# Low parts of the channel-stage weights: a negated copy by ScalarE and an adding DMA from GpSimd

## The chip, the core and the metric

The kernel runs on one core of one Trainium2 chip. TensorE multiplies matrices, VectorE (DVE) and ScalarE (ACT) do element-wise work, GpSimd (POOL) does element-wise work and can issue DMAs, SyncE (SP) issues DMAs. The metric is the device time of one execution in microseconds. A time is given as the median of several runs.

## What is computed

One layer of a decoder for 1024 prompt tokens and 8 x 4 sample tokens, 1056 in all, with 1024 features: a mixing stage (attention and pooling), a channel stage (a gated feed-forward layer with 2816 hidden features) and a last projection with a gate. The change touches the channel stage and the last projection. Cut to what matters:

```python
f = _rms(x, n_ffn_pre)
f = (jax.nn.silu(f @ w_gate) * (f @ w_up)) @ w_down
x = x + _rms(f, n_ffn_post)
x = x + jax.nn.sigmoid(x @ w_ple_gate) * (p @ w_ple)
```

All inputs and outputs are float32.

## The kernel before, in words

**Split operands.** TensorE multiplies in float32r, a rounded form of float32. To keep float32 accuracy, each operand is split in a high part (the value rounded to float32r) and a low part (the value minus its high part). A product takes three matmuls (`gemm`): high weight by high data, high weight by low data, low weight by high data, in this order for every block of 128 rows. The low weight, `wl`, is thus first read by the third matmul of its product. `split` (L163) makes the two parts: ScalarE copies the high part (L164), VectorE subtracts it from the source (L165).

**Groups.** The 1056 tokens are cut in three groups of 352 columns, 0, 1 and 2. A product of 1024 rows takes 24 matmuls of 128x352, one of 512 rows takes 12.

**Weights.** Weights are listed in `plan`, each a tile of 128 partitions x 1024 values, 512 KB. `w_load` has SyncE load one into a raw tile `wr`, of which there are three (`W_RAW`). `w_split` loads it, takes two `wp` tiles called `wh` and `wl`, and splits it. There are eight `wp` tiles (2 x `W_PAIRS`), so four pairs; a tile is written again only when TensorE has used what it held.

**Items.** From the channel stage on, weights are handed out by `ITEMS` and `need`. `need(k)` prepares all items up to `k + LOOK` (`LOOK` is 4) and loads the next two raw. An item is either "direct", one weight split as it is, or "sums": four GpSimd instructions (`w_sums`, L980) form sums of the quarters of a gate and an up weight in place, in their raw tiles, and two splits turn the results into tiles `sh` and `sl`, which also come from the `wp` tiles. With the sums, groups 0 and 1 share products and need fewer matmuls. The items hold 113 direct weights: 64 loads of `w_gu` (gate and up), 32 of `w_dn` (down), 14 of `w_pg` and 3 of `w_ple` (last projection). The 22 sums make 44 `sh`/`sl` pairs.

**Order of the work.** The hidden features are cut in 11 slabs of two chunks; a chunk is called a channel below. `WALK` goes over slabs 0 to 4 for group 2 alone, then slabs 5 to 10 for all three groups, then slabs 0 to 4 again for groups 0 and 1; the weights of slabs 0 to 4 are loaded and split twice. Meanwhile `ffn_steps` prepares groups 0 and 1 in the first part. `gate_up` does one channel; `down` multiplies a slab by its two down weights and adds the result into `o` (L1075, L1077). At the end `ple_out` does the last projection. From the attention's end on, TensorE's instructions stand in an order fixed by the program (`keep_in_program_order`); the other engines' orders follow from a scheduler. Each engine takes its queue in order, and an instruction that waits holds all behind it. In the channel stage GpSimd's queue has only the sums, and SyncE's has all weight loads.

`weights`, which serves the mixing stage, also calls `w_split`; its weights keep VectorE's subtraction in both kernels.

Of the kernel before, what the change touches and what calls it, by code (L numbers as in the profile page):

```python
# [12 lines left out]
AF = mybir.ActivationFunctionType  # L13
ALU = mybir.AluOpType
# [47 lines left out]
def trunk_kernel(  # L62
# [32 lines left out]
    te, ve, se, ge = nc.tensor, nc.vector, nc.scalar, nc.gpsimd  # L95
# [58 lines left out]
    plan = []  # L154
# [3 lines left out]
    def fix(ins):  # L158

        if fixed[0]:  # L160
            tc.keep_in_program_order(ins)

    def split(hi, lo, src):  # L163
        fix(se.copy(hi, src))  # L164
        fix(ve.tensor_tensor(lo, src, hi.bitcast(F32), op=ALU.subtract))  # L165

    raws, pairs = {}, {}

    def w_load(j):
        if j >= len(plan) or j in raws:  # L170
            return
        src, shape = plan[j]
        t = wpool.tile(shape, F32, tag="wr", bufs=W_RAW, name=nm("wr"))
        nc.sync.dma_start(t, src)
        raws[j] = t

    def w_tile(shape, s):
        return wpool.tile(shape, F32R, tag="wp", bufs=2 * W_PAIRS, name=nm(s))

    def w_split(j):  # L180
        if j >= len(plan) or j in pairs:
            return
        w_load(j)
        shape = plan[j][1]
        hi, lo = w_tile(shape, "wh"), w_tile(shape, "wl")
        split(hi, lo, raws[j])
        pairs[j] = (hi, lo)

    def weights(j, ahead=W_PAIRS - 1):
        for i in range(j, j + ahead + 1):  # L190
            w_split(i)
            w_load(i + 1)
        return pairs[j]
# [22 lines left out]
    def item(kind, *js):  # L216
        ITEMS.append((kind, js))
        return len(ITEMS) - 1
# [5 lines left out]
    for s, gs in WALK:  # L224
        pairs_of = []
        for i in range(SLAB):
# [9 lines left out]
            js = item("sums", jg, ju) if 0 in gs else None  # L236
# [25 lines left out]
    def need(k, ahead=LOOK):  # L262

        for i in range(len(made), min(k + ahead + 1, len(ITEMS))):
            kind, js = ITEMS[i]
            if kind == "direct":
                w_split(js[0])
                made[i] = pairs[js[0]]
            else:
                made[i] = w_sums(*(raws[ITEMS[j][1][0]] for j in js))  # L270
            for kind, js in ITEMS[i + 1 : i + 3]:
                if kind == "direct":
                    w_load(js[0])
        return made[k]
# [679 lines left out]
    for m in range(4, KC):  # L954
        out_proj(m, 1)
        need(0, m - 4)
        turn(24)
# [12 lines left out]
    def w_sums(a1, a2):  # L970


        a11, a12, a21, a22 = a1[:, 0:4, :], a1[:, 4:8, :], a2[:, 0:4, :], a2[:, 4:8, :]
        for out, a, b, op in (
            (a22, a21, a22, ALU.add),
            (a21, a11, a21, ALU.subtract),
            (a11, a22, a11, ALU.subtract),
            (a12, a12, a11, ALU.subtract),
        ):
            ge.tensor_tensor(out, a, b, op=op)  # L980
        two = []
        for src in (a1, a2):
            hl = w_tile([P, KC, P], "sh"), w_tile([P, KC, P], "sl")
            split(*hl, src)
            two.append(hl)
        (s24, s31) = two
        return {"S2": quarter(s24, 0), "S4": quarter(s24, 1), "S3": quarter(s31, 0), "S1": quarter(s31, 1)}
# [8 lines left out]
    def gate_up(items, slot, gs, pending):  # L996
# [16 lines left out]
        def add(out, a, ps):  # L1013
            ve.tensor_tensor(out, a, ps, op=ALU.add)  # L1014

        wg = need(ig)
        if 0 in gs:
            p1 = tmp(n, "p1")
# [8 lines left out]
        if pending and 0 in gs:  # L1027
            pending()
        wu = need(iu)
        if 2 in gs:  # L1030
            ve.tensor_tensor(sl, sl, direct(wu), op=ALU.mult)
# [234 lines left out]
```

## Time and profile before

| What | Value |
|---|---|
| Median of three runs | 1124.63 us (1122.67 to 1124.66) |
| Profiled execution, its own time | 1121.84 us |
| Its span, first to last instruction | 1120.1 us |
| TensorE busy | 1108.9 us |
| VectorE busy | 748.4 us |
| ScalarE busy | 440.7 us |
| GpSimd busy | 179.5 us |
| Read from device memory | 88.30 MB |

Engine times are taken from one profiled execution. In the page and the views, a row of a group gives line, engine, operation, output and input tiles with the buffer numbers left out, shape, count, and after the bar the busy time in us, the mean of one in ns, and the engine's idle time before them with what ended it. "PE b L126 <- DVE o L1107: 1.2, 1, 1.2" reads: TensorE, writing b at line 126, waited for VectorE's o of line 1107; us in total, times, longest. A row of the windows gives the window, its length, the busy time and count of each engine in it, the granted TensorE clock, the mean busy share of the 16 DMA engines, and GB/s. A row of the timeline gives start and length in us, engine, line and operation, and in brackets the idle time before it. A row of DMA issues gives out and in, the queue, the count, the KB of one, and the median us from issue to landing; the DMA queue's row gives packets, MB, and the time of its packets as a share of 16 engines' span. A source row gives shortest, median and longest in ns, and the first and last start in us.

### The profile page before, as it was taken

The page shows a single profiled execution, that of the slowest core. Times are in us where ns is not written, and L with a number is a line of the kernel's source. Part 1 is how long each engine was busy: PE and PEld are TensorE (multiplying, and loading weights), DVE is VectorE, ACT ScalarE, POOL GpSimd, SP SyncE. Part 2 cuts the span into 40 slices and gives each one's busy share as a digit, 9 for nine tenths or more (in the row PEclk, how much of TensorE's full clock was granted, in tenths as well). Part 3 has the DMA queues.
Part 4 walks back from the last instruction along what each step waited for, and adds up shares of the span by engine and source line. Part 5 has one row for each costly group of instructions (what it writes and reads, how often), then busy time and mean ns, then how long its engine had stood idle before and what let it go on. Part 6 is the DMA issues. An engine that isn't in the chain of part 4 may idle for free.

```text
span 1120.1 us, 17702 instructions
## 1 busy us (share of the span) xinstructions
PE 1108.9 (99%) x7171; PEld 1090.8 (97%) x7171; DVE 748.4 (67%) x1244; ACT 440.7 (39%) x782; POOL 179.5 (16%) x152
## 2 busy tenths in 40 slices
PE   8999999999999999999999999999999999999998
PEld 8999988899999999999999999999999999999998
DVE  6667468985879955355554555557887877789532
ACT  8323276664646524331321314124424334366220
POOL 0045132200000041011111101111132123100000
PEclk9999999999999999999999999999999999999999
DMA  8121311272543312111110212112212222246211
GB/s 288 57 70 43 119 41 38 83 265 71 206 159 132 114 38 76 39 61 54 38 57 20 75 38 76 39 39 93 104 57 77 74 76 79 96 161 215 91 58 39
DMA packets 35265, 99.54 MB, mean 89 GB/s; under 512 B 4180, under 2 KB 14708, under 8 KB 35184
## 3 DMA queue, kind: packets, MB, share of 16 engines
q1 hardware_dynamic: 33856, 96.65, 25.6%
q10 hardware_dynamic: 1328, 1.77, 0.5%
q8 instruction: 56, 0.92, 0.4%
q14 instruction: 25, 0.20, 0.1%
HBM read 88.30 MB, written 10.11 MB: 88 GB/s over the span
## 4 chain that ended last, share of the span: by engine, by line
PE 88%; DVE 6%; ACT 3%; DMA 1%; issue 1%; POOL 0%; SPq 0%; DVEq 0%; ACTq 0%; POOLq 0%
PE b L126 88%; ACT a L634 1%; DVE wl L165 1%; DMA xr<-in_x_dram 1%; DVE mx L626 1%; DVE a L671 1%; ACT wh L164 1%; POOL wr L980 0%; DVE h L366 0%; PE b L120 0%; DMA c<-in_gains_dram 0%; DVE o L1107 0%; DVE x L1111 0%; DVE a L734 0%; DVE p L1014 0%
## 5 line engine op out<-in xcount | busy, mean ns | idle before, releaser
L126 PE MATMUL b<-fh,wh 128*128 128x352 f32 x808 | 260.7, 323 | 0.0
L126 PE MATMUL b<-fh,wl 128*128 128x352 f32 x808 | 259.3, 321 | 0.0
L126 PE MATMUL b<-fl,wh 128*128 128x352 f32 x808 | 259.0, 321 | 0.0
L126 PE MATMUL b<-hid,wh 128*128 128x352 f32 x1056 | 252.5, 322 | 1.7 <-DVE o L1107 1.2
L164 ACT CAST wh<-wr 128x1024 fp32r<-128x1024 f32 (+1 forms) x139 | 142.9, 1030 | 249.6 <-PE b L126 206.6
L165 DVE TENSOR_TENSOR wl<-wr,wh 128x1024 fp32r<-128x1024 f32 (+1 forms) x139 | 171.7, 1238 | 63.8 <-ACT wh L164 63.6
L126 PEld LDWEIGHTS b<-hid,wh 128*128 128x128 f32 x1056 | 182.3, 188 | 2.5 <-issue 1.5
L126 PE MATMUL b<-hid,wl 128*128 128x352 f32 x528 | 169.0, 320 | 0.0
L980 POOL TENSOR_TENSOR wr<-wr 128x512 f32<-128x512 f32 x44 | 63.4, 1441 | 622.3 <-DVE wl L165 451.8
L126 PEld LDWEIGHTS b<-fl,wh 128*128 128x128 f32 x808 | 151.8, 188 | 0.0
L126 PEld LDWEIGHTS b<-fh,wl 128*128 128x128 f32 x808 | 151.8, 188 | 0.0
L126 PEld LDWEIGHTS b<-fh,wh 128*128 128x128 f32 x808 | 151.6, 188 | 0.0
L1077 DVE TENSOR_TENSOR o<-o,b 128x352 f32<-128x352 f32 x240 | 114.7, 514 | 27.3 <-PE b L126 27.2
L126 PE MATMUL b<-fh,sh 128*128 128x352 f32 x352 | 113.6, 323 | 0.0
L126 PE MATMUL b<-fl,sh 128*128 128x352 f32 x352 | 112.8, 320 | 0.0
L126 PE MATMUL b<-fh,sl 128*128 128x352 f32 x352 | 112.7, 320 | 0.0
L126 PE MATMUL b<-h,wh 128*128 128x352 f32 x480 | 106.1, 327 | 1.3 <-ACT h L364 0.9
L165 DVE TENSOR_TENSOR sl<-wr,sh 128x1024 fp32r<-128x1024 f32 x44 | 53.7, 1222 | 75.5 <-ACT sh L164 75.5
L126 PEld LDWEIGHTS b<-hid,wl 128*128 128x128 f32 x528 | 99.0, 187 | 0.0
L164 ACT CAST sh<-wr 128x1024 fp32r<-128x1024 f32 x44 | 45.7, 1047 | 130.9 <-POOL wr L980 91.3
L126 PEld LDWEIGHTS b<-h,wh 128*128 128x128 f32 x480 | 82.6, 190 | 2.6 <-DVE h L366 1.3
L126 PE MATMUL b<-h,wl 128*128 128x352 f32 x240 | 66.3, 325 | 0.0
(150 smaller groups left out, 1593.3 us busy)
## 6 DMA issues: line engine op xcount, KB each, us to landing
wr<-in_w_gu_dram SPq DMA_DIRECT2D x64, 512.0 KB, 3.3
wr<-in_w_dn_dram SPq DMA_DIRECT2D x32, 512.0 KB, 3.5
wr<-in_w_pg_dram SPq DMA_DIRECT2D x14, 512.0 KB, 3.7
x<-in_x_dram SPq DMA_DIRECT2D x6, 704.0 KB, 7.7
x1d<-x SPq DMA_DIRECT2D x6, 704.0 KB, 3.5
x<-x1d SPq DMA_DIRECT2D x6, 704.0 KB, 6.2
out_y_dram<-yo SPq DMA_DIRECT2D x24, 176.0 KB, 1.8
wr<-in_w_out_b_dram SPq DMA_DIRECT2D x8, 512.0 KB, 3.3
```

The lines of the kernel that those rows point to most:

```text
L126: ins = te.matmul(*args, **kw)
L164: fix(se.copy(hi, src))
L165: fix(ve.tensor_tensor(lo, src, hi.bitcast(F32), op=ALU.subtract))
L626: ve.tensor_reduce(mx, t, axis=AX.X, op=ALU.max)
L634: se.activation(t[:, c, :], t[:, c, :], AF.Exp, bias=nmx[:, c : c + 1], scale=scale, accum_out=sm[:, c : c + 1])
L671: ve.copy_predicated(tk, m4(0).bitcast(mybir.dt.int32), v4(cur[kv]))
L980: ge.tensor_tensor(out, a, b, op=op)
L1077: ve.tensor_tensor(o, o, v, op=ALU.add)
```

## The change

`w_split` gets a second way, used by every direct item of `need`, 113 weights: ScalarE copies the high part, then writes the negated raw weight, rounded, into the low tile; then a DMA issued by GpSimd reads the weight from device memory again and adds it onto what lies in the low tile. The rounded negated weight is the negated high part, so the sum is the low part. VectorE's subtraction is gone for these weights. The sums (`sh`, `sl`) and the mixing stage keep it. The raw load into `wr` stays, and TensorE's instructions and their order are the same. In GpSimd's queue the 113 DMA issues stand among the sums: the issue of a channel's up weight comes ahead of that channel's four sums.

```diff
--- before.py
+++ after.py
@@ -177,13 +177,19 @@
     def w_tile(shape, s):
         return wpool.tile(shape, F32R, tag="wp", bufs=2 * W_PAIRS, name=nm(s))
 
-    def w_split(j):
+    def w_split(j, by_dma=False):
         if j >= len(plan) or j in pairs:
             return
         w_load(j)
         shape = plan[j][1]
         hi, lo = w_tile(shape, "wh"), w_tile(shape, "wl")
-        split(hi, lo, raws[j])
+        if by_dma:
+
+            se.copy(hi, raws[j])
+            se.activation(lo, raws[j], AF.Copy, scale=-1.0)
+            ge.dma_start(lo, plan[j][0], accum_op=ALU.add)
+        else:
+            split(hi, lo, raws[j])
         pairs[j] = (hi, lo)
 
     def weights(j, ahead=W_PAIRS - 1):
@@ -264,7 +270,7 @@
         for i in range(len(made), min(k + ahead + 1, len(ITEMS))):
             kind, js = ITEMS[i]
             if kind == "direct":
-                w_split(js[0])
+                w_split(js[0], True)
                 made[i] = pairs[js[0]]
             else:
                 made[i] = w_sums(*(raws[ITEMS[j][1][0]] for j in js))
```

## The prediction

> **What bounds the kernel now.** I read the page first: busy times, then the chain that ended last.
>
> ```profile
> span 1120.1 us, 17702 instructions
> PE 1108.9 (99%) x7171; PEld 1090.8 (97%) x7171; DVE 748.4 (67%) x1244; ACT 440.7 (39%) x782; POOL 179.5 (16%) x152
> PE 88%; DVE 6%; ACT 3%; DMA 1%; issue 1%; POOL 0%; SPq 0%; DVEq 0%; ACTq 0%; POOLq 0%
> q1 hardware_dynamic: 33856, 96.65, 25.6%
> ```
>
> TensorE is busy in all but 11.2 us and holds 88% of the chain. The change adds and removes no matmul and leaves their order alone, so it can win only waits of TensorE, and it loses when a low part arrives after TensorE wants it. Next come the windows, cut where the walk over the slabs changes: from 264 slabs of group 2 alone ("first part"), from 403 all three groups, from 760 groups 0 and 1 ("third part"), from 1003 the last projection.
>
> ```profile
> core 0: us, PE busy (x) PEld busy (x) DVE busy (x) ACT busy (x) POOL busy (x), PEclk, DMA share, GB/s
> 264.00:403.00 139.00, 139.00 (x890) 138.88 (x889) 117.19 (x158) 75.50 (x96) 8.44 (x4) 1.00 0.41 137
> 403.00:760.00 357.00, 357.00 (x2249) 357.00 (x2248) 191.41 (x316) 99.28 (x152) 58.53 (x44) 1.00 0.15 50
> 760.00:1003.00 243.00, 241.19 (x1520) 240.17 (x1518) 193.98 (x315) 96.79 (x139) 55.57 (x40) 1.00 0.27 88
> 1003.00:1120.00 117.00, 112.19 (x702) 111.65 (x702) 63.99 (x99) 34.95 (x51) 0.00 (x0) 0.99 0.31 110
> PE b L126 <- DVE o L1107: 1.2, 1, 1.2
> PE b L126 <- DVE hid L165: 0.5, 1, 0.5
> PE b L126 <- DVE dg L310: 0.4, 1, 0.4
> ```
>
> The last three rows are all of TensorE's waits from 264 on: 2.1 us, each ended by VectorE, and the granted clock is 0.99 to 1.00. So **the most that a freed VectorE can give is 2.1 us**, 0.19% of the time, even if every one of these waits goes.
>
> **What is removed.** The 113 subtractions of direct weights leave VectorE:
>
> ```profile
> L165 DVE TENSOR_TENSOR wl<-wr,wh 128x1024 fp32r<-128x1024 f32 x113 | 137.6, 1220 | 48.8 <-ACT wh L164 48.6
> L164 ACT CAST wh<-wr 128x1024 fp32r<-128x1024 f32 x113 | 118.5, 1049 | 214.3 <-PE b L126 177.5 <-issue 31.7 <-DMA wr<-in_w_pg_dram 2.7
> ```
>
> VectorE loses 137.6 us that lay under TensorE. I put the gain at 0; its bounds are 0 and 2.1 us.
>
> **What is added on ScalarE.** 113 more passes over 128x1024. The nearest row is the high-part copy above, 1.05 us (a multiplying pass and a copy are alike at 1408 columns: 1377 and 1371 ns):
>
> ```profile
> L893 ACT ACTIVATE y<-x 128x1408 f32<-128x1408 f32 x4 | 5.5, 1377 | 0.7 <-DVE x L892 0.7
> L164 ACT CAST fh<-y 128x1408 fp32r<-128x1408 f32 x9 | 12.3, 1371 | 2.6 <-DVE y L939 1.8 <-DVE y L903 0.8
> ```
>
> That is 118.5 us, at most 32 x 1.05 = 34 us on 75.5 of 139 in the first part, where 32 of the weights are split. ScalarE has the room. What is queued behind a negated copy (a SiLU, a copy out of PSUM) is 1.05 us later; the eight banks in rotation take that up, since each is filled by 12 or 24 matmuls of 139.00/890 = 0.156 us (1.9 or 3.7 us). Cost 0; without that cover, up to 1 us a channel.
>
> **What is added on the DMA engines.** Each weight is now read twice: the plain load into wr stays, and the adding transfer reads the same 512 KB again. From the first fence, 25.6% of 1120.1 us moved 96.65 MB, 2.97 us per MB, so a plain 512 KB (0.524 MB) fills all 16 engines for 1.56 us. No adding transfer is in the trace. Its lower bound is 1.56 us, as a load. It must also read what lies in wl, and then write: if none of these three passes overlaps, 3 x 1.56 = 4.7 us. I take two, 3.1 us: a plain load reads and writes within its 1.56, so only the second read is extra. In the first part the engines were busy 0.41 x 139 = 57 us. With 32 more transfers this becomes 57 + 50 = 107, 57 + 99 = 156, or 57 + 150 = 207 us of 139. At my value the engines fall 17 us behind. The cover found below (11.7 us from ScalarE's start to first use, less a need of 9.5) takes 2 to 3 of these: **14 us lost in the first part**, bounds 0 and 66. In the second (0.15) and third (0.27) parts the engines stay under full even at 4.7 us: 34 weights each, 34 x 4.7 = 160 us on 66 of 243 in the third.
>
> The Trainium skill (Collectives: The Full Stack, The bandwidth ceiling) says that an adding DMA runs at half a copy's rate because both its sources are read through one ring, 62.28 against 32.35 GB/s. By that ratio of 1.93 the transfer takes 3.0 us here and the first part loses 11 instead of 14. No run here shows it yet.
>
> **What is added in time to arrival.** The rings set the cover: four pairs of wp tiles, so a high part can start only when the pair four places back has been used. These rows are ScalarE's start on wh and TensorE's first read of the matching wl (the third matmul of its product):
>
> ```profile
> 312.91 1.06 ACT L164 CAST wh<-wr 128x1024 fp32r<-128x1024 f32 x1 [1.14 <-issue]
> 324.59 0.32 PE L126 MATMUL b<-hid,wl 128*128 128x352 f32 x1
> ...
> 606.66 1.06 ACT L164 CAST wh<-wr 128x1024 fp32r<-128x1024 f32 x1 [4.56 <-PE b L126]
> 618.34 0.32 PE L126 MATMUL b<-fh,wl 128*128 128x352 f32 x1
> ...
> 757.29 1.05 ACT L164 CAST wh<-wr 128x1024 fp32r<-128x1024 f32 x1 [4.56 <-PE b L126]
> 765.15 0.32 PE L126 MATMUL b<-hid,wl 128*128 128x352 f32 x1
> ...
> 848.14 1.05 ACT L164 CAST wh<-wr 128x1024 fp32r<-128x1024 f32 x1
> 855.07 0.32 PE L126 MATMUL b<-fh,wl 128*128 128x352 f32 x1
> ...
> 891.70 1.04 ACT L164 CAST wh<-wr 128x1024 fp32r<-128x1024 f32 x1
> 898.46 0.32 PE L126 MATMUL b<-fh,wl 128*128 128x352 f32 x1
> ...
> 932.22 1.04 ACT L164 CAST wh<-wr 128x1024 fp32r<-128x1024 f32 x1
> 940.41 0.32 PE L126 MATMUL b<-fh,wl 128*128 128x352 f32 x1
> ...
> 980.57 1.05 ACT L164 CAST wh<-wr 128x1024 fp32r<-128x1024 f32 x1
> 987.12 0.32 PE L126 MATMUL b<-hid,wl 128*128 128x352 f32 x1
> ...
> 1014.01 1.04 ACT L164 CAST wh<-wr 128x1024 fp32r<-128x1024 f32 x1
> 1020.46 0.32 PE L126 MATMUL b<-fh,wl 128*128 128x352 f32 x1
> ```
>
> The first two pairs are typical of the first and second parts, 11.7 us. The other six are the tight places: 7.9, 6.9, 6.8, 8.2, 6.5 and 6.5 us. Before, wl needed 1.05 + 1.22 us. Now it needs two passes of ScalarE, 2.1 us, and then the time from GpSimd's issue to landing. Rows near that:
>
> ```profile
> wr<-in_w_gu_dram SPq DMA_DIRECT2D x64, 512.0 KB, 3.3
> x<-in_x_dram SPq DMA_DIRECT2D x6, 704.0 KB, 7.7
> L980 POOL TENSOR_TENSOR wr<-wr 128x512 f32<-128x512 f32 x44 | 63.4, 1441 | 622.3 <-DVE wl L165 451.8 <-DMA wr<-in_w_gu_dram 168.8
> ```
>
> The load of this size lands after 3.3 us. I add 1.56 for the second read, 1.0 for GpSimd to issue (not in the trace; from below 0, from above one of its 1.44 us instructions), and 1.56 for a plain load sharing the engines: 7.4 us, close to the 7.7 of the loads that queue behind others. The need is 2.1 + 7.4 = 9.5 us. The six places are short by 1.6, 2.6, 2.7, 1.3, 3.0 and 3.0: **14 us lost at the tight places**. The low bound is 3.3 + 1.0 = 4.3, need 6.4, nothing lost. The high bound is three passes beside a load, 3.3 + 3.1 + 1.0 + 1.56 = 9.0, need 11.1: short by 3.2, 4.2, 4.3, 2.9, 4.6 and 4.6, 24 us.
>
> **What is queued behind the waiting issue.** GpSimd takes its queue in order, so its four sums of a channel (L980, now L986) stand behind the issue of that channel's up weight, which waits for the negated copy. They needed VectorE's subtraction before (1.22), ScalarE's pass now (1.05), so they start 0.2 us earlier plus the issue, 1.0: 0.8 late. The cover is in the third part:
>
> ```profile
> 970.51 1.23 DVE L165 TENSOR_TENSOR sl<-wr,sh 128x1024 fp32r<-128x1024 f32 x1 [1.84 <-ACT sh L164]
> 974.73 0.32 PE L126 MATMUL b<-fh,sl 128*128 128x352 f32 x1
> ```
>
> From 971.74 to 974.73 is 3.0 us, so it costs nothing until an issue holds GpSimd for 3.2 us. The wr tile of a down or last-projection weight comes free 0.2 us earlier; SyncE's next load gains nothing that TensorE sees.
>
> **The sum.** 14 + 14 = 28 us, all of it waits of TensorE. The profiled execution took 1121.8 us (its span and 1.7 around it) and becomes 1150. The median shown, 1124.6, is 2.8 above that execution, so I forecast 1153.
>
> **Rivals.**
> *Hidden.* An adding transfer costs little more than a load: landing 4.3 us, 1.56 us of engines. It decides below a need of 6.5, where none of the eight pairs is late and the first part's engines hold 107 of 139 us. Then only VectorE's relief is left: 1122.5 to 1124.6, faster than before if all three waits go. For it: DMA share 0.15 to 0.41, covers mostly 11.7 us. Against: something must read the old wl. The Trainium skill (DMA: Bandwidth & Descriptors, Anatomy of one DMA) fits a GpSimd-issued DMA as 2.0 us plus bytes over 436 GB/s; plain that is 3.2 (the trace has 3.3 from SyncE), with twice the bytes 4.4 and 2.4 of engine time, which would fit this case: 57 + 77 = 134 of 139.
> *Three passes.* 66 + 24 = 90 us: 1215. For it: a transfer that reads, adds and writes back may overlap nothing. Against: plain loads do overlap reading with writing.
> *GpSimd holds each issue long*, say 6 us, writing the transfer. Sums are late by 2.8 in the third part's ten channels, 28 us; landing becomes 12.4, need 14.5: in the first part 2.8 us at every fourth of 32 weights, 22 us, and at the six places 6.6, 7.6, 7.7, 6.3, 8.0 and 8.0, 44 us: 1219. For it: GpSimd is slow (1.44 us for a half-tile sum). Against: SyncE issues the like in 0.33 us.
>
> ```profile
> L174 SPq DMA_DIRECT2D wr<-in_w_gu_dram x61: 327/328/328, 267.4 to 950.8; - x61
> ```
>
> **How the numbers follow.** A difference under 0.2%, 2.2 us, can't be told from none. Chances: forecast 0.52 (own range 1128 to 1185: landing 5.5 to 8.5 us, engines 2 to 3.8 us), hidden 0.14, three passes 0.24, held issue 0.10. Hidden splits into 0.04 faster, 0.07 same and 0.03 slower; all else is slower: 0.04, 0.07, 0.89. The range runs from 1126, a need of 6.9 with the first part hidden, to 1225, just past the two slow rivals; about 0.1 lies below and 0.1 above.
>
> **What would show it.** Right: L126 waits on a DMA of wl, most between 264 and 403 with the DMA share near 1, and again near the six places; landing about 7 us; VectorE some 138 us less, ScalarE 118 us more. Wrong: no waits on wl (hidden); waits of about equal size through 403 to 760 (landing over 9.6 us); sl late with GpSimd busy before it (held issue); a longer matmul where nothing waits.

## The result, and the profile after

| | Before | After |
|---|---|---|
| Median of four runs | 1123.78 us (1122.67 to 1124.66) | 1165.43 us (1164.06 to 1175.34) |
| Ratio of times, 95% interval | | 1.039 (1.035 to 1.043) |
| Profiled execution, its own time | 1121.84 us | 1166.63 us |
| Its span | 1120.1 us | 1164.9 us |

The change made the kernel slower by 41.7 us. The forecast was 1153, within 1126 to 1225: the sign and the range held, the size was 12 us short. First the page of the kernel after, the lines that answer to those of before:

```profile
span 1164.9 us, 18006 instructions
PE 1126.2 (97%) x7171; PEld 1102.6 (95%) x7171; DVE 646.8 (56%) x1131; ACT 543.3 (47%) x895; POOL 276.4 (24%) x265
q0 software_dynamic: 16272, 59.25, 28.1%
issue 46%; PE 27%; POOL 15%; DVE 4%; DMA 4%; ACT 3%; POOLq 0%; SPq 0%; ACTq 0%; DVEq 0%
```

TensorE ran the same 7171 matmuls, but they took 17.3 us longer (1126.2 against 1108.9), and its idle time grew from 11.2 to 38.7 us. So there are two losses to look for: waits, and matmuls that were themselves slower. The queue q0 is new: 113 adding transfers, 0.281 x 1164.9 / 113 = 2.90 us of all 16 engines each. The chain of waits is of little use here: 46% of it is "issue", time for which the profile shows no reason, since it wanders into GpSimd's queue. TensorE is still busy 97% of the span, so its own waits and its windows are the views to trust.

The windows of the kernel after, cut at the same moments as before, except that the last is longer:

```profile
core 0: us, PE busy (x) PEld busy (x) DVE busy (x) ACT busy (x) POOL busy (x), PEclk, DMA share, GB/s
264.00:403.00 139.00, 131.97 (x821) 129.30 (x820) 79.16 (x121) 99.04 (x120) 26.96 (x31) 0.99 0.97 249
403.00:760.00 357.00, 357.00 (x2233) 357.00 (x2232) 170.28 (x277) 126.74 (x182) 92.55 (x81) 1.00 0.44 98
760.00:1003.00 243.00, 233.43 (x1450) 230.72 (x1449) 148.66 (x251) 115.52 (x153) 81.30 (x71) 1.00 0.60 142
1003.00:1164.00 161.00, 144.85 (x871) 142.81 (x869) 67.86 (x126) 67.84 (x95) 16.45 (x19) 0.95 0.65 165
```

In the first part the DMA share went from 0.41 to 0.97: the engines are full, and TensorE is idle for 7.0 us. In the second part TensorE is busy without a gap. In the third it misses 9.6 us, in the last window 16 (4.8 before, with the same tail behind the last matmul), and there the granted clock is 0.95. These are TensorE's longest waits, grouped by what ended them:

```profile
PE b L126 <- DMA wl<-in_w_dn_dram: 9.0, 7, 2.8
PE b L126 <- DMA wl<-in_w_pg_dram: 8.1, 2, 5.4
PE b L126 <- DMA wl<-in_w_gu_dram: 6.2, 6, 2.6
PE b L126 <- DVE dg L316: 2.8, 2, 1.8
PE b L126 <- DMA wl<-in_w_ple_dram: 2.6, 1, 2.6
```

Sixteen waits on the adding transfer, 25.9 us; before there was none on a DMA. The DMA issues of the kernel after (the last number is the median from issue to landing), with the store `x1d` as a bystander:

```profile
wr<-in_w_gu_dram SPq DMA_DIRECT2D x64, 512.0 KB, 4.9
wl<-in_w_gu_dram POOLq DMA_DIRECT2D x64, 512.0 KB, 7.0
wl<-in_w_dn_dram POOLq DMA_DIRECT2D x32, 512.0 KB, 8.7
wl<-in_w_pg_dram POOLq DMA_DIRECT2D x14, 512.0 KB, 8.2
x1d<-x SPq DMA_DIRECT2D x6, 704.0 KB, 13.6
```

An adding transfer lands after 7.0 to 8.7 us, and plain loads suffer with it: 4.9 us where the same load took 3.3. ScalarE waits 29.5 us in all for plain loads of `w_gu` and `w_dn` before its high-part copies (0.5 in the kernel before), which shortens the cover of what it then splits.

**Where the 44.8 us between the two profiled spans arise.** Both programs give TensorE the same instructions in the same order, so the n-th matmul on a split weight can be set beside the n-th of before, and the difference of their starts tells how late TensorE runs. Its growth, worked out from the timelines of both traces, with before's times as borders of the parts (980 rather than 1003, so that the tight place at 980.57 falls to the end), is:

```
growth of the lateness, us     first 264-403   second 403-760   third 760-980   end 980-1115
kernel after                       11.2             2.5             10.7            18.5
forecast                           14               0                8.2             6
```

Another 1.8 us lie before 264, where the two programs do the same work. The forecast's fourteen at tight places are 8.2 in the third part and 6.0 at the end. Three of four parts came out within 3 us; the end is 12.5 us too small, which is most of the 16.6 us by which the forecast for the profiled execution, 1150, fell short.

The forecast took all of its 28 us to be waits of TensorE. The waits on `wl` are 25.9 us, but not where they were put: 6.8 in the first part (14 forecast), 8.4 in the third (8.2) and 10.7 at the end (6). The other 19 us are losses that no term of the sum had; they are taken apart below.

### The profile page after: what moved, and what is told of

Its sections match the earlier page's. It is cut to its first block, busy times and chain, and to the rows that moved or that the text cites. A ratio compares the mean times of both kernels' runs of the same rounds, so it can differ in the third digit from the quotient of the medians.

```text
span 1164.9 us, 18006 instructions
## 1 busy us (share of the span) xinstructions
PE 1126.2 (97%) x7171; PEld 1102.6 (95%) x7171; DVE 646.8 (56%) x1131; ACT 543.3 (47%) x895; POOL 276.4 (24%) x265
## 4 chain that ended last, share of the span: by engine, by line
issue 46%; PE 27%; POOL 15%; DVE 4%; DMA 4%; ACT 3%; POOLq 0%; SPq 0%; ACTq 0%; DVEq 0%
PE b L126 27%; POOL wr L986 10%; POOL wl L190 5%; DMA wl<-in_w_pg_dram 2%; DMA wl<-in_w_dn_dram 2%; ACT a L640 1%; DMA xr<-in_x_dram 1%; DVE wl L165 1%; DVE mx L632 1%; DVE a L677 1%; DVE acc L789 0%; ACT wh L164 0%; DMA c<-in_gains_dram 0%; DVE h L372 0%; PE b L120 0%
## 5 line engine op out<-in xcount | busy, mean ns | idle before, releaser
L126 PE MATMUL b<-fh,wl 128*128 128x352 f32 x808 | 264.5, 327 | 14.4 <-DMA wl<-in_w_pg_dram 8.1
L126 PE MATMUL b<-fh,wh 128*128 128x352 f32 x808 | 263.9, 327 | 0.0
L126 PE MATMUL b<-fl,wh 128*128 128x352 f32 x808 | 262.4, 325 | 0.0
L188 ACT CAST wh<-wr 128x1024 fp32r<-128x1024 f32 x113 | 118.4, 1048 | 227.8 <-PE b L126 175.5
L126 PEld LDWEIGHTS b<-fh,wl 128*128 128x128 f32 x808 | 155.1, 192 | 17.3 <-DMA wl<-in_w_pg_dram 8.7
L190 POOL DMA_DIRECT2D wl<-in_w_gu_dram x64 | 56.0, 874 | 458.6 <-ACT wl L189 408.4
L126 PEld LDWEIGHTS b<-fl,wh 128*128 128x128 f32 x808 | 154.6, 191 | 0.0
L126 PEld LDWEIGHTS b<-fh,wh 128*128 128x128 f32 x808 | 154.3, 191 | 0.0
L189 ACT ACTIVATE wl<-wr 128x1024 fp32r<-128x1024 f32 x113 | 119.1, 1054 | 0.0
L126 PEld LDWEIGHTS b<-hid,wl 128*128 128x128 f32 x528 | 99.6, 189 | 11.8 <-DMA wl<-in_w_dn_dram 11.7
L986 POOL TENSOR_TENSOR wr<-wr 128x512 f32<-128x512 f32 x44 | 66.1, 1502 | 1.7
## 6 DMA issues: line engine op xcount, KB each, us to landing
x1d<-x SPq DMA_DIRECT2D x6, 704.0 KB, 13.6
```

Source lines behind the costliest of these rows:

```text
L126: ins = te.matmul(*args, **kw)
L188: se.copy(hi, raws[j])
L189: se.activation(lo, raws[j], AF.Copy, scale=-1.0)
L190: ge.dma_start(lo, plan[j][0], accum_op=ALU.add)
```

## The experiments

Each kernel is the changed one with the edit shown; its time is compared with before's median on the same chip, which lay between 1122.61 and 1124.82 us, and the interval of the ratio is 95%. Four restrict the adding DMA to parts of the walk; all other direct weights get VectorE's subtraction back. `PART[k]` is the number of items before entry k of `WALK`; `AHEAD` is the end of the first part and `NSLAB` that of the second.

### One part at a time

**First part alone.**

```diff
-                w_split(js[0], True)
+                w_split(js[0], i < PART[AHEAD])
```

> The adding DMA serves only the 30 direct weights of the first part of the walk (group 2 alone); all later direct weights keep VectorE's subtraction. Transfer theory (16 DMA engines full in the first part, late arrival in the third part and at the end, and the lower clock after those waits): 10 to 13 us over the kernel before, 1134 to 1137 us, DMA share above 0.9 between 264 and 403 and no wait on wl after 420. ScalarE theory (its second pass over each weight is what delays): about 30/113 of the 42 us, 11 us, but with TensorE waits ended by ScalarE and spread evenly.

Measured: 1132.29 us, 1.0076 (1.0061 to 1.0091), 8.5 us more. TensorE waits three times on `wl`, 5.5 us; in the lateness the first part grew by 9.0 and the rest by less than 0.3. The loss is real, if smaller than the 10 to 13 us that I expected (the edit reaches 28 weights, not 30), and what is lost there isn't won back later.

**Second part alone.**

```diff
-                w_split(js[0], True)
+                w_split(js[0], PART[AHEAD] <= i < PART[NSLAB])
```

> The adding DMA serves only the direct weights of the second part (all three groups). Transfer theory: no TensorE wait on wl at all, 1123 to 1127 us; the upper end if the 0.65% longer matmuls of that part in the changed kernel come from the transfers, the lower end if they came with that execution. ScalarE theory: 34/113 of 42 us, 12 us, so 1136.

Measured: 1123.6 us, 1.000 (0.999 to 1.001). The DMA issues of this kernel:

```profile
wl<-in_w_gu_dram POOLq DMA_DIRECT2D x24, 512.0 KB, 5.9
wl<-in_w_dn_dram POOLq DMA_DIRECT2D x12, 512.0 KB, 8.8
```

And its second part's window:

```profile
403.00:760.00 357.00, 357.00 (x2249) 357.00 (x2248) 173.30 (x281) 127.58 (x182) 87.02 (x76) 1.00 0.42 97
```

Thirty-six transfers, whose median landing goes up to 8.8 us, cost nothing where the cover is 11.7 us and the engines have room, and the same 2249 matmuls as before fit in the window. It also shows what a freer VectorE is worth in this part: nothing.

**Third part and end.**

```diff
-                w_split(js[0], True)
+                w_split(js[0], i >= PART[NSLAB])
```

> The adding DMA serves only the direct weights of the third part and of the last projection. Transfer theory: 26 to 32 us over the kernel before, 1150 to 1156, with single waits of 1 to 5 us on wl and lower granted clock after 1003. ScalarE theory: about 49/113 of 42 us, 18 us, 1142. If the three single-part kernels add up to 42 us, the parts do not feed each other.

Measured: 1154.12 us, 1.0273 (1.0244 to 1.0301), 30.4 us more: 20.5 us of waits on `wl`, and 17 us in which the granted clock was one half (in part of it TensorE still waited, as is shown below for the changed kernel). The three parts nearly add: 8.5 + 0 + 30.4 = 38.9 of 41.7 us.

**Third part without the end.**

```diff
-                w_split(js[0], True)
+                w_split(js[0], PART[NSLAB] <= i < PART[-1])
```

> The adding DMA serves only the third part, without the last two down weights and the last projection. If the parts do not feed each other: 10 to 12 us, 1134 to 1136, which leaves 19 of the 30 us of the third-part-and-end kernel to the end. If the end's waits come from what the third part leaves behind in the queues: more than 15 us, waits on DMAs after 980 although no weight there is added onto.

Measured: 1136.11 us, 1.0118 (1.0103 to 1.0133), 13.5 us more, just over what I expected; of it 9.1 in six waits on `wl`, of which those of 1.82 and 2.45 us were each followed by 3.4 us at half clock. After 980 nothing more is lost, so the third part alone leaves nothing behind for the end: the other 30.4 - 13.5 = 16.9 us arise at the end. A kernel that changes the end alone was not run.

### What the transfer costs

**Copy in place of add.** The low part then holds the whole weight, so the kernel computes something else; only its time counts.

```diff
-            ge.dma_start(lo, plan[j][0], accum_op=ALU.add)
+            ge.dma_start(lo, plan[j][0])
```

> The GpSimd DMA copies the weight over the low tile instead of adding onto it, so the low part holds the whole weight; path, issue and order are those of the changed kernel. If the second read of an adding transfer is the price: engines 1.5 to 1.6 us for a transfer instead of 2.9, landing 4.5 to 5.5 us instead of 7 to 9, no wait in the first part (107 of 139 us) and under 3 us in all: 1123 to 1128. If the issue from GpSimd and its fixed time are the price: landing stays over 6.5 us and 1145 or more.

Measured: 1136.67 us, 1.0109 (1.0080 to 1.0138). The adding queue's row on the page of this kernel, now a copying one, and its DMA issues:

```profile
q0 software_dynamic: 16272, 59.25, 15.8%
wl<-in_w_gu_dram POOLq DMA_DIRECT2D x64, 512.0 KB, 4.2
```

Its window of the first part:

```profile
264.00:403.00 139.00, 139.00 (x890) 138.77 (x889) 84.66 (x129) 103.68 (x127) 22.36 (x36) 1.00 0.76 260
```

And TensorE's longest wait on the copies, by group:

```profile
PE b L126 <- DMA wl<-in_w_pg_dram: 5.1, 2, 3.9
```

A copy takes 0.158 x 1133.0 / 113 = 1.58 us of the engines, a plain load's 1.56; the addition doubles it, lengthens the median landing from 4.2 to 7.0 us for `w_gu` and is worth 29.8 us (41.7 over before for the change, 11.9 for this kernel). The first part then loses nothing and the third 1.4 us. But the end still loses 11 us: there even a copy is late, though its need, 2.1 + 5.0 (the landing of a `w_pg` copy) = 7.1 us, should miss the cover of 6.5 by 0.6. The miss of the expectation lies there: the copy behind the wait of 3.9 us, issued at 1022.6, landed after 8.2 us, not 5.0.

**Add from the raw tile in SBUF** rather than from device memory.

```diff
-            ge.dma_start(lo, plan[j][0], accum_op=ALU.add)
+            ge.dma_start(lo, raws[j], accum_op=ALU.add)
```

> The adding DMA reads the raw tile on the chip instead of device memory; the raw tile then stays taken until the transfer lands. If reading device memory twice is the price: engine time and landing fall to those of a copy, 1124 to 1132. If two reads are the price wherever they come from: engine time near 2.9 us again, and with three raw tiles held some 7 us longer the plain loads come later, 1165 to 1200.

Measured: 1237.01 us, 1.0998 (1.0973 to 1.1024). The adding queue's row on its page:

```profile
q0 software_dynamic: 16272, 59.25, 26.2%
```

And TensorE's two longest groups of waits:

```profile
PE b L126 <- DMA wl<-wr: 27.1, 19, 4.7
PE b L126 <- DVE o L1083: 24.3, 11, 4.0
```

A transfer takes 0.262 x 1232.2 / 113 = 2.86 us, like the 2.90 of the add from device memory. So adding doubles the engines' time wherever its source lies. That a second read is the reason fits this, but no run separates reading from adding. The kernel is slowest of all, and slower than the 1165 to 1200 that I expected: the raw tile is now held until the transfer has landed, so SyncE's next loads wait for these transfers, 77 times and 484 us in all, and ScalarE waits 107 us for the loads.

**The traffic without the data path.** VectorE splits as before, and an adding DMA of the same size, from the finished low part to a buffer in device memory that nobody reads, runs beside it.

```diff
-            se.copy(hi, raws[j])
-            se.activation(lo, raws[j], AF.Copy, scale=-1.0)
-            ge.dma_start(lo, plan[j][0], accum_op=ALU.add)
+            split(hi, lo, raws[j])
+            spare.append(dpool.tile([P, *shape[1:]], F32, name=nm("spare")))
+            ge.dma_start(spare[-1], lo.bitcast(F32), accum_op=ALU.add)
```

> VectorE's subtraction makes the low part as before; besides, GpSimd issues an adding DMA of 512 KB for each direct weight, from the finished low part onto a buffer in device memory that nothing reads. So the engines' load is there and no product waits for it. If late arrival through the ring is what costs: nothing outside the first part, and there only what the plain loads are late by, 0 to 8 us, 1124 to 1132. If the load on the engines alone costs (the plain loads come late): 20 us or more, TensorE waiting behind ScalarE's wait on wr.

Measured: 1153.04 us, 1.0262 (1.0237 to 1.0287). ScalarE's waits on loads in this kernel:

```profile
ACT wh L164 <- DMA wr<-in_w_gu_dram: 40.6, 22, 4.3
ACT wh L164 <- DMA wr<-in_w_dn_dram: 11.5, 6, 3.2
```

No matmul waits for these transfers, and 28 us are lost all the same: the plain loads come late (before, ScalarE waited 0.5 us for loads of `w_gu` and `w_dn`, here 52.1), and once VectorE waits 2.6 us for a low slot that a transfer still reads. I had expected 0 to 8 us; the load on the engines counts for more than the forecast allowed outside the first part. It isn't the changed kernel's loss taken alone, since a low slot here is held by VectorE's pass and the transfer together.

**Half a transfer.** The DMA adds onto the first half of the low tile; VectorE subtracts in the other.

```diff
-            se.activation(lo, raws[j], AF.Copy, scale=-1.0)
-            ge.dma_start(lo, plan[j][0], accum_op=ALU.add)
+            n = shape[1] // 2
+            se.activation(lo[:, :n], raws[j][:, :n], AF.Copy, scale=-1.0)
+            ge.dma_start(lo[:, :n], plan[j][0][:, :n], accum_op=ALU.add)
+            ve.tensor_tensor(lo[:, n:], raws[j][:, n:], hi[:, n:].bitcast(F32), op=ALU.subtract)
```

> Only the first half of each low tile is made by the negated copy and the adding DMA; VectorE subtracts the second half. Transfer theory: the time follows the size of the transfer. Engines 1.4 to 1.5 us each, so the first part is not full (57 + 28 x 1.45 = 98 of 139 us) and loses nothing; landing 5.5 to 6 us, need about 7.4, so places with 6.5 to 6.9 us of cover are short by 0.5 to 0.9 and no wait is long enough to lower the clock: 1125 to 1131. If a fixed price of each issue from GpSimd or of each ScalarE pass decides, half a transfer costs nearly what a whole one does: 1145 or more.

Measured: 1145.52 us, 1.0207 (1.0187 to 1.0226). TensorE's waits:

```profile
PE b L126 <- DVE o L1085: 5.4, 3, 2.5
PE b L126 <- DMA wl<-in_w_pg_dram: 3.4, 2, 2.5
PE b L126 <- DVE hid L165: 1.7, 1, 1.7
```

The first part loses next to nothing (0.3 us), as a transfer of 1.57 us of the engines should. The rest is a miss of my theory: waits on `wl` fell to 5.3 us, but new waits on VectorE, 5.4 and 1.7 us, came in their place, and 13.7 us passed at half clock. Splitting the work over three engines brought new waits here rather than removing them.

### What ScalarE's pass costs

**The pass without the DMA.** ScalarE writes the negated copy, VectorE adds the raw weight.

```diff
-            ge.dma_start(lo, plan[j][0], accum_op=ALU.add)
+            ve.tensor_tensor(lo, raws[j], lo.bitcast(F32), op=ALU.add)
```

> ScalarE writes the negated copy as in the changed kernel, but VectorE then adds the raw weight onto it; there is no second transfer. Transfer theory: 0 to 3 us over the kernel before (need 2.1 + 1.2 us against covers of 6.5 and more), 1124 to 1127, ScalarE some 118 us busier. ScalarE theory: most of the 42 us stays, 1150 or more.

Measured: 1136.2 us, 1.0101 (1.0082 to 1.0121). The group of VectorE's additions in this kernel:

```profile
L190 DVE TENSOR_TENSOR wl<-wr,wl 128x1024 fp32r<-128x1024 f32 x113 | 138.3, 1224 | 93.7 <-ACT wl L189 93.4
```

And TensorE's waits:

```profile
PE b L126 <- DVE o L1083: 4.5, 3, 2.3
PE b L126 <- DVE hid L165: 2.8, 2, 2.6
```

The pass isn't free in general: 11.4 us, where I expected 0 to 3. But, as far as these waits show, the mechanism is one that the changed kernel doesn't have. VectorE stands 93.4 us before its additions, waiting for ScalarE's second pass (48.6 before, for the first), and holds the work for `o` and `hid` behind it. In the changed kernel VectorE has no low part to wait with, and TensorE's waits on those two together are 1.2 us.

**Negated copy and issue first.**

```diff
-            se.copy(hi, raws[j])
             se.activation(lo, raws[j], AF.Copy, scale=-1.0)
             ge.dma_start(lo, plan[j][0], accum_op=ALU.add)
+            se.copy(hi, raws[j])
```

> ScalarE writes the negated copy and GpSimd's issue follows before ScalarE copies the high part, so each adding transfer starts about 1.05 us earlier and nothing else changes. Transfer theory: each wait of the third part and the end is about 1 us shorter, the first part stays (its engines are full): 1148 to 1158. ScalarE theory: the same work on ScalarE, no gain, 1163 to 1167.

Measured: 1159.89 us, 1.0327 (1.0310 to 1.0345), 36.1 us over before where the change has 41.7, so some 5.5 us less, a little less of a gain than I expected. Waits on `wl` fell from 25.9 to 13.7 us; in their place:

```profile
PE b L126 <- DVE o L1083: 3.6, 4, 1.3
PE b L126 <- DVE hid L165: 2.3, 4, 0.6
```

So 1.05 us on the way to the landing is worth 12 us of those waits, and 5.9 us of waits on VectorE's `o` and `hid` give half of it back.

**High part by VectorE**, so that ScalarE has one pass only.

```diff
-            se.copy(hi, raws[j])
+            ve.tensor_copy(hi, raws[j])
```

> VectorE copies the high part, ScalarE only writes the negated copy, so ScalarE makes one pass for each weight as in the kernel before and the adding transfer is issued 1.05 us earlier than in the changed kernel. Transfer theory: the first part still loses 8 to 11 us, the third part and the end lose 1 us less at each of their 8 to 10 waits: 1150 to 1158. If the second pass in ScalarE's queue is the larger half of the loss: 1140 or less. If no gain over 1162: neither, and the copy on VectorE holds GpSimd up.

Measured: 1159.86 us, 1.0337 (1.0319 to 1.0354), 37.3 us over before, some 4.4 us less than the change, which the intervals don't quite tell apart; I expected more. VectorE's copy takes 0.69 us; landing stays at 7.5 to 9.1 us, and 21.8 us of waits on `wl` remain. By these two kernels ScalarE's extra pass is worth some 5 us in the changed kernel. That the adding makes most of the rest is shown by the copy in place of it, which took away 29.8. None of these kernels beats the one before; the only one that equals it uses the adding DMA in the second part alone.

## Why the forecast was right, and where it was short

**TensorE bounds, and a freed VectorE gives nothing.** Held. VectorE's busy time fell by 101.6 us and no time came back: where the DMA cost nothing, in the second part alone, the time is 1123.6.

**ScalarE's passes cost nothing.** Nearly. The row is 1054 ns x 113 = 119.1 us, as forecast (ScalarE's busy time rose by 102.6 only, since passes that follow each other overlap by 0.1 us), and no wait of the changed kernel names them. Taking a pass out of the transfer's way won 4.4 to 5.5 us, in two ways; the forecast had this pass in its need of 2.1 us.

**The engines fill in the first part.** Held. I took two reads, 3.1 us; the page shows 2.90, a copy 1.58, an add from SBUF 2.86. The share of 0.97 is the full engine that 156 us of work in 139 foretold, and 11.2 us were lost (8.5 alone) where 14 were forecast. The forecast had them all as waits; the waits are 6.8. The lateness arises in two ways: the adding transfer lands after 8.8 us in the median, and the plain loads are late too. Ahead of this part's longest wait, 2.77 us at 336, ScalarE had waited 4.29 us for a load of `w_dn`, so the cover there was 7.2 us instead of 11.7. The Trainium skill (Collectives: The Full Stack, The bandwidth ceiling) gave a ratio of 1.93 between copy and add, by which, as an estimate, the transfer takes 3.0 us and 11 us are lost; it states this for a collective among four ranks. The trace has 2.90 / 1.58 = 1.84, which is near it.

**Landing of 7.4 us, 1.0 of it the issue.** Held as a median over all places, 7.0 us for `w_gu`, 8.2 for `w_pg` and 8.7 for `w_dn`, but not place by place. By parts, shortest, median and longest are 7.1, 8.8 and 13.2 us in the first, 5.2, 7.2 and 10.4 in the second, 5.2, 6.3 and 9.5 in the third, and 7.7, 8.5 and 12.2 between 1003 and 1071. One value for all places was the weak step of the sum, as the next paragraphs show. The issue has a row of its own in the kernel after:

```profile
L190 POOL DMA_DIRECT2D wl<-in_w_gu_dram x64 | 56.0, 874 | 458.6 <-ACT wl L189 408.4
```

0.87 us each. The fit in the Trainium skill (DMA: Bandwidth & Descriptors, Anatomy of one DMA) would have given, as an estimate with the bytes counted twice, 4.4 us to landing and 2.4 of the engines; the shortest landing here is 5.2 us, and the engines take 2.90.

**The sums behind the issue cost nothing.** Held: none of TensorE's waits is on `sh` or `sl`. The held issue of 6 us and the three passes are excluded by 0.87 and 2.90 us, and the hidden transfer by sixteen waits.

**The tight places of the third part.** The sum held, but by luck. At the four listed places, forecast to be short by 1.6, 2.6, 2.7 and 1.3 us, TensorE waited 0.70, 1.23, 1.44 and 0.18: 3.6 us instead of 8.2, because these transfers landed after 5.5 to 6.4 us rather than 7.4. Another 4.8 us came at four places that I hadn't listed: 1.07, 1.38, 1.12 and 1.25 us, each on a down weight whose transfer was issued about 2 us behind another adding transfer and landed after 8.6 to 9.2 us. Their covers before were 11.6, 9.4, 9.2 and 10.5 us, two of them under my own need of 9.5. One of the four:

```profile
917.35 0.86 POOL L190 DMA_DIRECT2D wl<-in_w_dn_dram  x1 [1.00 <-ACT wl L189]
...
926.21 0.43 PE L126 MATMUL b<-hid,wl 128*128 128x352 f32 x1 [1.12 <-DMA wl<-in_w_dn_dram]
```

So a landing that was too long at one kind of place and too short at the other gave 8.4 us of waits for 8.2. The lateness grew by 10.7: one more wait, of 1.2 us, is on VectorE's `o`, and the rest is spacing.

**The end: the term that was mis-sized.** "The six places are short by 1.6, 2.6, 2.7, 1.3, 3.0 and 3.0": the last two, 6 us, became 18.5. The step that failed is the landing of 7.4 us, taken to hold at the end too. One place was right: the matmul at 1020.46 of before waits. The other, at 987.12, doesn't; two that I hadn't listed come just ahead, and their waits, 5.3 us, delay it. The timeline of before has their covers:

```profile
974.17 1.05 ACT L164 CAST wh<-wr 128x1024 fp32r<-128x1024 f32 x1
975.68 1.04 ACT L164 CAST wh<-wr 128x1024 fp32r<-128x1024 f32 x1
...
982.36 0.32 PE L126 MATMUL b<-pl,wl 128*128 128x352 f32 x1
...
983.31 0.32 PE L126 MATMUL b<-fh,wl 128*128 128x352 f32 x1
```

8.2 and 7.6 us against a need of 9.5 would have been short by 1.3 and 1.9, 3.2 in place of 3.0: the omission hardly moved the sum. What moved it stands in the timeline of the kernel after, where the same three matmuls come at 1011.37, 1015.29 and 1063.60 (each with ScalarE's first pass, GpSimd's issue, and the wait):

```profile
1003.29 0.89 POOL L190 DMA_DIRECT2D wl<-in_w_ple_dram  x1 [7.07 <-ACT wl L189]
1011.37 0.43 PE L126 MATMUL b<-pl,wl 128*128 128x352 f32 x1 [2.57 <-DMA wl<-in_w_ple_dram]
...
1005.57 0.86 POOL L190 DMA_DIRECT2D wl<-in_w_pg_dram  x1 [1.40 <-ACT wl L189]
1015.29 0.66 PE L126 MATMUL b<-fh,wl 128*128 128x352 f32 x1 [2.70 <-DMA wl<-in_w_pg_dram]
...
1051.45 1.04 ACT L188 CAST wh<-wr 128x1024 fp32r<-128x1024 f32 x1
1053.75 0.86 POOL L190 DMA_DIRECT2D wl<-in_w_pg_dram  x1 [4.07 <-ACT wl L189]
1063.60 0.66 PE L126 MATMUL b<-fh,wl 128*128 128x352 f32 x1 [5.40 <-DMA wl<-in_w_pg_dram]
1064.06 0.50 PE L126 MATMUL b<-fh,wh 128*128 128x352 f32 x1
1064.36 0.50 PE L126 MATMUL b<-fl,wh 128*128 128x352 f32 x1
```

From issue to the matmul it is 8.1, 9.7 and 9.9 us, not 7.4. For the last, the need from ScalarE's start is 1063.60 - 1051.45 = 12.2 us and the cover 12.2 - 5.4 = 6.8, close to before's 6.5. The waits are 2.57 + 2.70 + 5.40 = 10.7 us, 4.7 more than the 6 forecast. The engines were full while these transfers were under way: the DMA share is 0.97 from 1003.3 to 1015.3 and 1.05 from 1053.7 to 1063.6. They share the engines with plain loads and with each other, for which the forecast had allowed one load's 1.56 us; it had looked for full engines in the three parts up to 1003, and not behind them. From 1120 to 1140, where the share is 0.67, three more transfers of `w_pg` landed after 5.4 to 6.6 us.

The rest was in no term of the sum. The last two rows above start 0.30 us apart, where two matmuls of this size normally start 0.16 apart: after its wait TensorE ran at half speed. Windows of 4 us of the kernel after, around the first part's wait that ends at 323.3 (2.58 us) and around this one (the columns are those above):

```profile
320.00:324.00 4.00, 1.43 (x9) 1.13 (x8) 0.00 (x0) 1.78 (x5) 0.86 (x1) 1.00 1.03 360
324.00:328.00 4.00, 4.00 (x17) 4.00 (x16) 0.00 (x0) 1.92 (x3) 0.00 (x0) 0.57 0.92 238
...
1062.00:1066.00 4.00, 2.40 (x8) 2.40 (x9) 1.04 (x2) 1.95 (x4) 0.86 (x1) 0.50 1.05 290
```

The granted clock is 0.57 behind the one wait and 0.50 behind the other. Finer windows place the half clock at 324.1 to 327.5 in the first part, and at 1013.6 to 1020.4, 1040.9 to 1044.3 and 1061.4 to 1068.2 at the end: 3.4 us, and 6.8, 3.4 and 6.8. From 264 to its last matmul, before has none. Two of these stretches begin while TensorE still waits, so it was busy for only 5.2, 3.4 and 4.6 us of the three at the end. Some 45 matmuls start there 0.29 us apart instead of 0.16, which loses about 6 us; in the first part it is 1.5. With the wait of 1.75 us on `dg` at 1039, 0.4 before, the end is 10.7 + 6 + 1.4 = 18.1 us, near the 18.5 by which the lateness grew. The third part has no such stretch, although it waits nine times: its waits are 1.44 us at most.

The Trainium skill (TensorE: Matmul & The Clock Gate, Part 1: The HAM clock gate) describes a half rate after an idle window of some 3.4 us and full rate after a busy one. The pieces of 3.4 and 6.8 us agree with its window; that the array must be idle for one whole window doesn't, since here waits of 1.75 to 2.6 us, with some matmuls near them, were enough.

Experiments bear out both parts of this. With a copy, whose landing is 5.0 us for a `w_pg` weight, the end loses 11 us rather than 18.5. With the third part alone nothing is lost after 980. That the late landings come from the traffic at the end, rather than from GpSimd's queue, is argued from the DMA share, from the later transfers of the same weights, and from the issue rows, each of which starts within 0.4 us of ScalarE's finish, so that the delay lies behind the issue; it wasn't tried by itself.

**The rest of the first part.** Of the 11.2 us, 6.8 are waits and 1.5 half clock. The other 2.9 are nearly all in the starts of single matmuls: behind each of the five waits the matmuls come 0.27 us later than the wait is long, 1.4 in all, and 1.2 us are delays of 0.1 to 0.4 at reads of `wl` between 299 and 312 and at 389, too short to be listed as waits.

**What stays open.** In the second part the changed kernel runs 2.5 us later without a wait. The loss is spread evenly: between 420 and 740 TensorE runs 2002 matmuls in the kernel after and 2016 before, 160.0 ns apart instead of 158.9. This is one of three steps that the spacing takes. The half transfer and the high part by VectorE have the 2002 too, the traffic beside has 1988 (161.1 ns), and the copy, the pass without the DMA and the second part alone have 2016. As the last of these has the same adding transfers there, the step isn't the price of the transfers; the end of the kernel before has spacings of 160.0 ns as well. What sets the step no run shows. (Two kernels have waits of their own in this part: negated copy first is 4.5 us later there, the add from the raw tile 21.6.)

## What to carry to other kernels

Before a slower way of making an operand takes the place of a faster one, list the cover of every slot of its ring, from the moment that the slot is free to the first use, stage by stage: the change here cost nothing where the cover was 11.7 us and the engines had room, 11 us where the same cover met full engines, and 17 to 18.5 us at the end, where it was 6.5 to 8.2. Look for full engines around each tight slot, and not only in the mean of a part: one landing time for all places gave the right sum in the third part by luck and the wrong one at the end. Count an adding DMA as two plain loads of the engines, whatever its source, and let no stage that is already loaded take it. And where TensorE bounds, price a wait of about 2 us or more higher than its length: at the end, matmuls at half clock cost about half as much again as the waits.

## What the runs showed of the hardware beyond the forecast

- TensorE waits of about 2 us can be followed by 3.4 or 6.8 us at half the granted clock. Not all are: 2.58 us at 323 was, 2.77 us at 336 wasn't, and at 1039 1.75 us on VectorE's `dg` were enough. With the third part alone, waits of 1.82 and 2.45 us were, and one of 1.75 wasn't.
- Adding transfers on GpSimd's queue slow the loads and stores that other queues issue. The store `x1d` of 704 KB landed after 3.5 us before, after 9.1 with copies in place of adds, and after 13.6 in the changed kernel; in the other kernels with whole adding transfers for all weights it took 7.8 to 11.2, so the adding alone doesn't set it.
- VectorE lost 101.6 us of busy time, not the 137.6 of the subtractions removed. Other work of VectorE got longer. Its subtraction `hid<-c,hid` of 128x352, else 0.52 us long, takes 2.41 us in all six places where it meets both GpSimd's issue and the sum behind it, as in these rows of the timeline of the kernel after, 0.98 beside a sum alone and 0.52 beside an issue alone; its mean is 1120 ns there and was 581 before. In the second part this is hidden.

```profile
427.58 0.86 POOL L190 DMA_DIRECT2D wl<-in_w_gu_dram  x1 [8.71 <-ACT wl L189]
427.74 2.42 DVE L165 TENSOR_TENSOR hid<-c,hid 128x352 fp32r<-128x352 f32 x1
```
